# Batched x·yᵀ for 96 heads: groups of four heads with a last tile stored in unequal partition counts, in place of groups of eight heads

## Chip, cores and metric

The kernel runs on one core of a Trainium2 chip. The metric is the device time of one execution in microseconds (us). The core has four compute engines, each with its own instruction queue: TensorE (PE, matrix products), VectorE (DVE) and ScalarE (ACT), which copy and cast, and GpSimd (POOL). SyncE (SP) issues all of this kernel's transfers between HBM and on-chip memory (SBUF); 16 DMA engines carry them out. Matrix products land in PSUM, from where DVE and ACT copy them to SBUF.

## What is computed

```python
def setup_inputs():
    batch, n_heads, seq_t, seq_s, channels = 8, 12, 512, 512, 64
    # x: (8, 12, 512, 64) float32, y: (8, 12, 512, 64) float32

def reference(x, y):
    return np.einsum('bhtc,bhsc->bhts', x, y).astype(np.float32)
```

For each of the 96 heads, a 512×64 matrix times the transpose of another: 512×512 float32 results. 12.6 MB of x and as much of y are read, and 100.7 MB are written.

## The kernel before

A group is eight heads, as two sets `a` of four. In a set, the 128 partitions hold four heads of 32 partitions each; a partition holds 16 consecutive rows of its head (`R`), so each transfer is contiguous in HBM.

**Loads.** `load(g)` (lines 52 to 57) brings 1 MB of y and 1 MB of x, as [128, 2, 16, 64] float32. Three groups are loaded ahead (`AHEAD`).

**`prepare(g)`** (lines 65 to 104) is a generator whose pieces are taken, one at a time, between the matmuls of the group before. POOL casts to bf16 in four instructions (line 73), and each cast puts the same row slot of set 0 and of set 1 side by side, 64 channels each. The next load is queued behind the casts (line 75), since it reuses their buffer. Then PE transposes: 16 slots of y (line 82) and 16 of x (line 95), each a full 128×128, so channels come to lie on partitions, set 0 on 0 to 63 and set 1 on 64 to 127. DVE and ACT copy the transposes from PSUM to `yT` and `xT` (lines 88, 90, 100, 102).

**Products** (lines 109 to 136). For each set, `ot` is a tile of 128 partitions × 16 rows × 512, 4 MB; three such tiles are in rotation. For every pair of row slots, eight matmuls (line 122), each 32 columns of `xT` against 512 of `yT`, fill two PSUM banks `pm`; ACT (line 129) and DVE (line 131) take turns in copying `pm` to `ot`.

**Stores.** A finished `ot` goes out in one DMA of 4 MB (line 136), 32 KB per partition. The first and the last tile go out in four DMAs of 1 MB each (line 134). All loads and stores are on SP's queue in program order. A DMA is issued when its data is there and when the DMA eight places before it, whose completion semaphore it uses again, has landed; the first eight have nothing to wait for in that respect.

Of the kernel before, what the change touches and what calls it, by code (L numbers as in the profile page):

```python
# [1 line left out]

# [5 lines left out]


@with_exitstack  # L10
def kernel(
    ctx: ExitStack,
    tc: tile.TileContext,
    x: bass.AP,
    y: bass.AP,
    out: bass.AP,
):

    nc = tc.nc
    B, H, T, C = x.shape
    _, _, S, _ = y.shape
    P = 128
    G = 4
    Q = P // G
    R = T // Q
    NG = B * H // (2 * G)  # L30
    K = R // 2
    AHEAD = 3
    fp32 = mybir.dt.float32
    bf16 = mybir.dt.bfloat16
    COPY = mybir.ActivationFunctionType.Copy
    assert C * 2 == P and S == T and R == 16

    xv = x.rearrange("b h t c -> (b h t c)").rearrange("(g a p n) -> g p a n", a=2, p=P, n=R * C)
    yv = y.rearrange("b h t c -> (b h t c)").rearrange("(g a p n) -> g p a n", a=2, p=P, n=R * C)
    ov = out.rearrange("b h t s -> (b h t s)").rearrange("(g a p n) -> g a p n", a=2, p=P, n=R * S)  # L40

    const = ctx.enter_context(tc.tile_pool(name="const", bufs=1))
    lpool = ctx.enter_context(tc.tile_pool(name="lpool", bufs=AHEAD))
    bpool = ctx.enter_context(tc.tile_pool(name="bpool", bufs=2))
    tpool = ctx.enter_context(tc.tile_pool(name="tpool", bufs=2))
    opool = ctx.enter_context(tc.tile_pool(name="opool", bufs=3))
    ptpool = ctx.enter_context(tc.tile_pool(name="ptpsum", bufs=2, space=bass.MemoryType.PSUM))
    pmpool = ctx.enter_context(tc.tile_pool(name="pmpsum", bufs=3, space=bass.MemoryType.PSUM))

    loaded = {}  # L50

    def load(g):
        xs = lpool.tile([P, 2, R, C], fp32)
        ys = lpool.tile([P, 2, R, C], fp32)
        nc.sync.dma_start(ys.rearrange("p a r c -> p a (r c)"), yv[g])  # L55
        nc.sync.dma_start(xs.rearrange("p a r c -> p a (r c)"), xv[g])
        loaded[g] = (xs, ys)

    for g in range(AHEAD):
        load(g)  # L60

    ident = const.tile([P, P], bf16)
    make_identity(nc, ident)

    def prepare(g, made):

        xs, ys = loaded.pop(g)
        yb = bpool.tile([P, R, 2, C], bf16)
        xb = bpool.tile([P, R, 2, C], bf16)
        for s, b in ((ys, yb), (xs, xb)):  # L70
            for half in range(2):
                rows = slice(half * K, (half + 1) * K)
                nc.gpsimd.tensor_copy(b[:, rows], s[:, :, rows].rearrange("p a r c -> p r a c"))  # L73
        if g + AHEAD < NG:
            load(g + AHEAD)
        yield
        yT = tpool.tile([P, G * Q, R], bf16)
        xT = tpool.tile([P, R, P], bf16)
        for half in range(2):
            pt = ptpool.tile([P, K, P], bf16)  # L80
            for k in range(K):
                nc.tensor.transpose(  # L82
                    pt[:, k, :], yb[:, half * K + k].rearrange("p a c -> p (a c)"), ident
                )
            dst = yT[:, :, half * K:(half + 1) * K]
            src = pt.rearrange("p k n -> p n k")
            if half == 0:
                nc.vector.tensor_copy(dst, src)  # L88
            else:
                nc.scalar.activation(dst, src, COPY)  # L90
            yield
        for half in range(2):
            pt = ptpool.tile([P, K, P], bf16)
            for k in range(K):
                nc.tensor.transpose(  # L95
                    pt[:, k, :], xb[:, half * K + k].rearrange("p a c -> p (a c)"), ident
                )
            dst = xT[:, half * K:(half + 1) * K]
            if half == 0:
                nc.vector.tensor_copy(dst, pt)  # L100
            else:
                nc.scalar.activation(dst, pt, COPY)  # L102
            yield
        made[g] = (xT, yT.rearrange("p n k -> p (n k)"))

    made = {}
    for _ in prepare(0, made):
        pass
    for g in range(NG):
        xT, yT = made.pop(g)  # L110
        steps = prepare(g + 1, made) if g + 1 < NG else iter(())
        for a in range(2):
            ot = opool.tile([P, R, S], fp32)
            otf = ot.rearrange("p r s -> p (r s)")
            edge = (g == 0 and a == 0) or (g == NG - 1 and a == 1)
            for k in range(K):
                if k in (0, 3, 6):
                    next(steps, None)
                pm = pmpool.tile([P, 2, S], fp32)
                for two in range(2):  # L120
                    for h in range(G):
                        nc.tensor.matmul(  # L122
                            pm[h * Q:(h + 1) * Q, two, :],
                            xT[a * C:(a + 1) * C, 2 * k + two, h * Q:(h + 1) * Q],
                            yT[a * C:(a + 1) * C, h * S:(h + 1) * S],
                            start=True, stop=True,
                        )
                if k % 2 == 0:
                    nc.scalar.activation(ot[:, 2 * k:2 * k + 2, :], pm, COPY)  # L129
                else:  # L130
                    nc.vector.tensor_copy(ot[:, 2 * k:2 * k + 2, :], pm)  # L131
                if edge and k % 2 == 1:
                    i, j = (2 * k - 2) * S, (2 * k + 2) * S
                    nc.sync.dma_start(ov[g, a][:, i:j], otf[:, i:j])
            if not edge:
                nc.sync.dma_start(ov[g, a], otf)  # L136


# [1 line left out]
_INS = ['x', 'y']  # L140
_OUTS = [((8, 12, 512, 512), 'float32')]


# [23 lines left out]
```

## Time and profile before

| | before |
|---|---|
| median of 3 runs | 307.4 us (307.38 to 307.46) |
| profiled execution, its time | 307.38 us |
| profiled execution, its span | 305.6 us |
| PE busy | 203.8 us, 67% |
| DVE busy | 138.4 us, 45% |
| ACT busy | 119.6 us, 39% |
| POOL busy | 49.3 us, 16% |
| bytes moved by DMA | 126.11 MB, mean 413 GB/s |
| DMA packets | 10867 |
| load issued to landed, median | 21.2 us (y), 23.4 us (x) |
| 4 MB store issued to landed, median | 27.4 us |

The span runs from the first to the last instruction; the time holds what lies around it as well. "Busy" of an engine is the sum of its instructions. The page cuts the span in 40 slices and gives for each the busy share of the 16 DMA engines and the rate. A group of instructions is shown with its line, engine, output and input, count, total busy time, mean duration in ns, and the idle time of its engine just before, with what ended most of it. The trace also holds each DMA packet with its start, duration and size, and for each DMA the moments at which its 16 parts landed; neither carries the number of the DMA engine.

### The profile page before, as it was taken

The numbers are of one execution on the slowest core, as the hardware profiler recorded it, in microseconds if no ns is written. First come the engines' busy times: TensorE is split into PE (matmuls) and PEld (weight loads), VectorE is DVE, ScalarE is ACT, GpSimd is POOL, SyncE is SP. The second block draws the span as 40 slices with busy tenths as digits, with TensorE's granted clock in tenths as the row PEclk, the third lists the DMA queues.
The fourth block names the chain that finished last, engine by engine and source line by source line (L and its number), as shares of the span: only waits on it lengthen the run. The fifth ranks groups of instructions, "written<-read, shape, count | busy, mean of one in ns | idle before, by whom it ended". The sixth has DMA issues, their size and how long they took to land.

```text
span 305.6 us, 4378 instructions
## 1 busy us (share of the span) xinstructions
PE 203.8 (67%) x1920; PEld 91.5 (30%) x1920; DVE 138.4 (45%) x120; ACT 119.6 (39%) x121; POOL 49.3 (16%) x54
## 2 busy tenths in 40 slices
PE   1899999969919928936932990991785976575000
PEld 1443234525404503512511540350251432222000
DVE  0465654657416507615633741670664664446000
ACT  1445527544523606505522451560653463325000
POOL 3755024300500500320140050041000000000000
PEclk9999999975555555755675555575575555555555
DMA  7999999999999999999999999999999999999980
GB/s 278 412 409 420 459 419 399 470 418 388 446 455 388 440 446 398 441 429 437 427 424 442 420 427 430 411 454 420 437 435 425 427 442 422 437 437 422 409 368 39
DMA packets 10867, 126.11 MB, mean 413 GB/s; under 512 B 864, under 2 KB 864, under 8 KB 7008
## 3 DMA queue, kind: packets, MB, share of 16 engines
q1 hardware_dynamic: 10848, 125.83, 97.2%
q8 instruction: 15, 0.25, 0.3%
q14 instruction: 4, 0.03, 0.0%
HBM read 25.17 MB, written 100.66 MB: 412 GB/s over the span
## 4 chain that ended last, share of the span: by engine, by line
DMA 49%; PE 29%; DVE 5%; issue 4%; ACT 3%; POOL 1%; SPq 0%; ACTq 0%
DMA out_dram<-ot 47%; PE pm L122 23%; DVE ot L131 5%; PE pt L95 4%; ACT ot L129 3%; PE pt L82 2%; DMA xs<-in_x_dram 2%; ACT xT L102 1%; POOL xb L73 1%; DVE xT L100 0%; SPq L55 0%; ACTq L129 0%; SPq L136 0%
## 5 line engine op out<-in xcount | busy, mean ns | idle before, releaser
L122 PE MATMUL pm<-yT,xT 64*32 64x512 bf16 x1536 | 159.4, 586 | 67.2 <-ACT ot L129 64.7
L131 DVE COPY ot<-pm 128x1024 f32<-128x1024 f32 x96 | 117.0, 1224 | 123.0 <-DMA out_dram<-ot 63.4
L129 ACT ACTIVATE ot<-pm 128x1024 f32<-128x1024 f32 x96 | 95.9, 1023 | 115.5 <-DMA out_dram<-ot 72.1
L122 PEld LDWEIGHTS <-xT 64*32 64x32 bf16 x1536 | 53.3, 118 | 148.1 <-issue 136.3
L73 POOL CAST yb<-ys 128x1024 bf16<-128x1024 f32 x24 | 24.3, 1040 | 143.5 <-PE pt L82 69.8
L82 PE MATMUL pt<-ident,yb 128*128 128x128 bf16 x192 | 23.9, 297 | 8.5 <-POOL yb L73 6.8
L102 ACT ACTIVATE xT<-pt 128x1024 bf16<-128x1024 bf16 x12 | 12.3, 1023 | 37.0 <-PE pt L95 30.3
L95 PE MATMUL pt<-ident,xb 128*128 128x128 bf16 x192 | 25.8, 310 | 1.3 <-DVE xT L100 0.8
L73 POOL CAST xb<-xs 128x1024 bf16<-128x1024 f32 x24 | 24.3, 1040 | 13.7 <-issue 4.9
L95 PEld LDWEIGHTS <-xb 128*128 128x128 bf16 x192 | 19.4, 143 | 22.7 <-issue 20.0
L82 PEld LDWEIGHTS <-yb 128*128 128x128 bf16 x192 | 19.3, 138 | 17.7 <-issue 8.2
L88 DVE COPY yT<-pt 128x1024 bf16<-128x1024 bf16 x12 | 14.6, 1216 | 8.5 <-PE pt L82 8.5
L90 ACT ACTIVATE yT<-pt 128x1024 bf16<-128x1024 bf16 x12 | 12.2, 1019 | 8.2 <-PE pt L82 8.2
L100 DVE COPY xT<-pt 128x1024 bf16<-128x1024 bf16 x12 | 8.3, 690 | 12.3 <-PE pt L95 9.8
L90 ACT ACT_TABLE_LOAD x1 | 1.3, 1283 | 0.7 <-PEq L151 0.7
masks.py:199 POOL TENSOR_SCALAR_AFFINE_SELECT ident<-ident 128x128 bf16<-128x128 bf16 x1 | 0.3, 292 | 0.1
masks.py:197 POOL MEMSET ident<- 128x128 bf16 x1 | 0.2, 204 | 0.3 <-POOLq L151 0.3
L151 POOL MEMSET const-float32-0.0<- 128x1 f32 x1 | 0.1, 98 | 0.2 <-issue 0.2
L151 POOL MEMSET const-bfloat16-1.0<- 128x1 bf16 x1 | 0.1, 101 | 0.0
L151 POOL MEMSET const-uint8-127<- 128x1 uint8 x1 | 0.1, 101 | 0.0
L151 POOL MEMSET const-float32-1.0<- 128x1 f32 x1 | 0.1, 98 | 0.0
## 6 DMA issues: line engine op xcount, KB each, us to landing
out_dram<-ot SPq DMA_DIRECT2D x22, 4096.0 KB, 27.4
ys<-in_y_dram SPq DMA_DIRECT2D x12, 1024.0 KB, 21.2
xs<-in_x_dram SPq DMA_DIRECT2D x12, 1024.0 KB, 23.4
out_dram<-ot SPq DMA_DIRECT2D x8, 1024.0 KB, 19.2
```

What stands on the lines that cost most here:

```text
L73: nc.gpsimd.tensor_copy(b[:, rows], s[:, :, rows].rearrange("p a r c -> p r a c"))
L82: nc.tensor.transpose(pt[:, k, :], yb[:, half * K + k].rearrange("p a c -> p (a c)"), ident)
L88: nc.vector.tensor_copy(dst, src)
L90: nc.scalar.activation(dst, src, COPY)
L95: nc.tensor.transpose(pt[:, k, :], xb[:, half * K + k].rearrange("p a c -> p (a c)"), ident)
L100: nc.vector.tensor_copy(dst, pt)
L102: nc.scalar.activation(dst, pt, COPY)
L122: nc.tensor.matmul(pm[h * Q:(h + 1) * Q, two, :], xT[a * C:(a + 1) * C, 2 * k + two, h * Q:(h + 1) * Q], yT[a * C:(a + 1) * C, h * S:(h + ...
L129: nc.scalar.activation(ot[:, 2 * k:2 * k + 2, :], pm, COPY)
L131: nc.vector.tensor_copy(ot[:, 2 * k:2 * k + 2, :], pm)
L151: nc = _bacc.Bacc("TRN2", target_bir_lowering=False, num_devices=1)
```

## The change

A group is now four heads (`NG` 24 in place of 12). The parts:

- **Loads** are 512 KB each, [128, 1024]; six groups are loaded ahead, with six buffers.
- **Casts.** y is cast in one instruction that writes each row's 64 channels twice, side by side (2048 elements per partition); x is cast as it lies.
- **Transposes.** 16 of y per four heads, each with the same 64 channels on partitions 0 to 63 and on 64 to 127; 8 of x per four heads, each of two consecutive row slots, the even one on partitions 0 to 63 and the odd one on 64 to 127. One DVE copy with a rearranged output writes `xT`, in place of one by DVE and one by ACT.
- **Products.** An `ot` holds two heads: 64 partitions each, 8 rows per partition, 2 MB; eight tiles in rotation. For a `pm`, four matmuls of 64 columns against 512.
- **Stores.** One DMA of 2 MB per tile, 16 KB per partition. The first tile goes out in two DMAs of 1 MB each. The last tile is cut by columns into four pieces of 3, 1, 1.5 and 2.5 times 512 elements; the second is one DMA over 128 partitions; the others are two DMAs each, over 120 and 8, 108 and 20, and 126 and 2 partitions.

```diff
-    NG = B * H // (2 * G)
+    NG = B * H // G
     K = R // 2
-    AHEAD = 3
+    HP = 2
+    I = R // 2
...
-    xv = x.rearrange("b h t c -> (b h t c)").rearrange("(g a p n) -> g p a n", a=2, p=P, n=R * C)
+    xv = x.rearrange("b h t c -> (b h t c)").rearrange("(g p n) -> g p n", p=P, n=R * C)
...
-    ov = out.rearrange("b h t s -> (b h t s)").rearrange("(g a p n) -> g a p n", a=2, p=P, n=R * S)
+    ov = out.rearrange("b h t s -> (b h t s)").rearrange("(g a p n) -> g a p n", a=G // HP, p=P, n=I * S)
...
-    lpool = ctx.enter_context(tc.tile_pool(name="lpool", bufs=AHEAD))
+    lpool = ctx.enter_context(tc.tile_pool(name="lpool", bufs=6))
...
-    opool = ctx.enter_context(tc.tile_pool(name="opool", bufs=3))
+    opool = ctx.enter_context(tc.tile_pool(name="opool", bufs=8))
...
     def load(g):
-        xs = lpool.tile([P, 2, R, C], fp32)
-        ys = lpool.tile([P, 2, R, C], fp32)
-        nc.sync.dma_start(ys.rearrange("p a r c -> p a (r c)"), yv[g])
-        nc.sync.dma_start(xs.rearrange("p a r c -> p a (r c)"), xv[g])
+        xs = lpool.tile([P, R * C], fp32)
+        ys = lpool.tile([P, R * C], fp32)
+        nc.sync.dma_start(ys, yv[g])
+        nc.sync.dma_start(xs, xv[g])
...
         yb = bpool.tile([P, R, 2, C], bf16)
-        xb = bpool.tile([P, R, 2, C], bf16)
-        for s, b in ((ys, yb), (xs, xb)):
-            for half in range(2):
-                rows = slice(half * K, (half + 1) * K)
-                nc.gpsimd.tensor_copy(b[:, rows], s[:, :, rows].rearrange("p a r c -> p r a c"))
-        if g + AHEAD < NG:
-            load(g + AHEAD)
+        nc.gpsimd.tensor_copy(
+            yb, ys.rearrange("p (r c) -> p r c", c=C).unsqueeze(2).to_broadcast([P, R, 2, C])
+        )
+        xb = bpool.tile([P, R * C], bf16)
+        nc.gpsimd.tensor_copy(xb, xs)
+        if g + 6 < NG:
+            load(g + 6)
...
-        xT = tpool.tile([P, R, P], bf16)
+        xT = tpool.tile([P, K // 2, P, 2], bf16)
...
-        for half in range(2):
-            pt = ptpool.tile([P, K, P], bf16)
-            for k in range(K):
-                nc.tensor.transpose(
-                    pt[:, k, :], xb[:, half * K + k].rearrange("p a c -> p (a c)"), ident
-                )
-            dst = xT[:, half * K:(half + 1) * K]
-            if half == 0:
-                nc.vector.tensor_copy(dst, pt)
-            else:
-                nc.scalar.activation(dst, pt, COPY)
-            yield
+        pt = ptpool.tile([P, K, P], bf16)
+        for k in range(K):
+            nc.tensor.transpose(pt[:, k, :], xb[:, k * P:(k + 1) * P], ident)
+        nc.vector.tensor_copy(
+            xT.rearrange("p i n e -> p i e n"), pt.rearrange("p (e i) n -> p i e n", e=2)
+        )
...
-        for a in range(2):
-            ot = opool.tile([P, R, S], fp32)
-            otf = ot.rearrange("p r s -> p (r s)")
-            edge = (g == 0 and a == 0) or (g == NG - 1 and a == 1)
-            for k in range(K):
-                if k in (0, 3, 6):
+        for hp in range(G // HP):
+            ot = opool.tile([P, I, S], fp32)
+            edge = (g == 0 and hp == 0) or (g == NG - 1 and hp == 1)
+            for i2 in range(I // 2):
+                if i2 % 2 == 0:
                     next(steps, None)
                 pm = pmpool.tile([P, 2, S], fp32)
-                for two in range(2):
-                    for h in range(G):
+                for h2 in range(HP):
+                    h = hp * HP + h2
+                    for par in range(2):
                         nc.tensor.matmul(
-                            pm[h * Q:(h + 1) * Q, two, :],
-                            xT[a * C:(a + 1) * C, 2 * k + two, h * Q:(h + 1) * Q],
-                            yT[a * C:(a + 1) * C, h * S:(h + 1) * S],
+                            pm[h2 * 64:(h2 + 1) * 64, par, :],
+                            xT[par * C:(par + 1) * C, i2, h * Q:(h + 1) * Q, :].rearrange("c q e -> c (q e)"),
+                            yT[par * C:(par + 1) * C, h * S:(h + 1) * S],
                             start=True, stop=True,
                         )
...
-                if edge and k % 2 == 1:
-                    i, j = (2 * k - 2) * S, (2 * k + 2) * S
-                    nc.sync.dma_start(ov[g, a][:, i:j], otf[:, i:j])
+                if edge and i2 % 2 == 1:
+                    otf = ot.rearrange("p r s -> p (r s)")
+                    if g == 0:
+                        cuts = [((2 * i2 - 2) * S, (2 * i2 + 2) * S, P)]
+                    elif i2 == 1:
+                        cuts = [(0, 3 * S, 120), (3 * S, 4 * S, P)]
+                    else:
+                        cuts = [(4 * S, 5 * S + S // 2, 108), (5 * S + S // 2, 8 * S, 126)]
+                    for a, b, n in cuts:
+                        nc.sync.dma_start(ov[g, hp][:n, a:b], otf[:n, a:b])
+                        if n < P:
+                            nc.sync.dma_start(ov[g, hp][n:, a:b], otf[n:, a:b])
             if not edge:
-                nc.sync.dma_start(ov[g, a], otf)
+                nc.sync.dma_start(ov[g, hp], ot.rearrange("p r s -> p (r s)"))
```

More of the change, by code (lines that the diff above doesn't have):

```diff
@@ L29 @@
     R = T // Q
-    NG = B * H // (2 * G)
+    NG = B * H // G
     K = R // 2
-    AHEAD = 3
+    HP = 2
+    I = R // 2
     fp32 = mybir.dt.float32
     bf16 = mybir.dt.bfloat16
-    COPY = mybir.ActivationFunctionType.Copy
     assert C * 2 == P and S == T and R == 16
-    xv = x.rearrange("b h t c -> (b h t c)").rearrange("(g a p n) -> g p a n", a=2, p=P, n=R * C)
-    yv = y.rearrange("b h t c -> (b h t c)").rearrange("(g a p n) -> g p a n", a=2, p=P, n=R * C)
-    ov = out.rearrange("b h t s -> (b h t s)").rearrange("(g a p n) -> g a p n", a=2, p=P, n=R * S)
+    xv = x.rearrange("b h t c -> (b h t c)").rearrange("(g p n) -> g p n", p=P, n=R * C)
+    yv = y.rearrange("b h t c -> (b h t c)").rearrange("(g p n) -> g p n", p=P, n=R * C)
+    ov = out.rearrange("b h t s -> (b h t s)").rearrange("(g a p n) -> g a p n", a=G // HP, p=P, n=I * S)
     const = ctx.enter_context(tc.tile_pool(name="const", bufs=1))
-    lpool = ctx.enter_context(tc.tile_pool(name="lpool", bufs=AHEAD))
+    lpool = ctx.enter_context(tc.tile_pool(name="lpool", bufs=6))
     bpool = ctx.enter_context(tc.tile_pool(name="bpool", bufs=2))
     tpool = ctx.enter_context(tc.tile_pool(name="tpool", bufs=2))
-    opool = ctx.enter_context(tc.tile_pool(name="opool", bufs=3))
+    opool = ctx.enter_context(tc.tile_pool(name="opool", bufs=8))
     ptpool = ctx.enter_context(tc.tile_pool(name="ptpsum", bufs=2, space=bass.MemoryType.PSUM))
@@ L52, in load @@
     def load(g):
-        xs = lpool.tile([P, 2, R, C], fp32)
-        ys = lpool.tile([P, 2, R, C], fp32)
-        nc.sync.dma_start(ys.rearrange("p a r c -> p a (r c)"), yv[g])
-        nc.sync.dma_start(xs.rearrange("p a r c -> p a (r c)"), xv[g])
+        xs = lpool.tile([P, R * C], fp32)
+        ys = lpool.tile([P, R * C], fp32)
+        nc.sync.dma_start(ys, yv[g])
+        nc.sync.dma_start(xs, xv[g])
         loaded[g] = (xs, ys)
-    for g in range(AHEAD):
+    for g in range(6):
         load(g)
@@ L89, in prepare @@
             else:
-                nc.scalar.activation(dst, src, COPY)
+                nc.scalar.activation(dst, src, mybir.ActivationFunctionType.Copy)
             yield
-        for half in range(2):
-            pt = ptpool.tile([P, K, P], bf16)
-            for k in range(K):
-                nc.tensor.transpose(
-                    pt[:, k, :], xb[:, half * K + k].rearrange("p a c -> p (a c)"), ident
-                )
-            dst = xT[:, half * K:(half + 1) * K]
-            if half == 0:
-                nc.vector.tensor_copy(dst, pt)
-            else:
-                nc.scalar.activation(dst, pt, COPY)
-            yield
+        pt = ptpool.tile([P, K, P], bf16)
[4 more added lines that the diff above has]
+        )
         made[g] = (xT, yT.rearrange("p n k -> p (n k)"))
+        yield
     made = {}
@@ L126 @@
                             start=True, stop=True,
                         )
-                if k % 2 == 0:
-                    nc.scalar.activation(ot[:, 2 * k:2 * k + 2, :], pm, COPY)
-                else:
-                    nc.vector.tensor_copy(ot[:, 2 * k:2 * k + 2, :], pm)
-                if edge and k % 2 == 1:
-                    i, j = (2 * k - 2) * S, (2 * k + 2) * S
-                    nc.sync.dma_start(ov[g, a][:, i:j], otf[:, i:j])
+                if i2 % 2 == 0:
+                    nc.scalar.activation(ot[:, 2 * i2:2 * i2 + 2, :], pm, mybir.ActivationFunctionType.Copy)
+                else:
+                    nc.vector.tensor_copy(ot[:, 2 * i2:2 * i2 + 2, :], pm)
```

## Prediction

> **What bounds the kernel now.** I read the page's part 2 and 3 first. Columns of part 2: the span in 40 slices, DMA share in tenths and GB/s.
>
> ```profile
> DMA  7999999999999999999999999999999999999980
> GB/s 278 412 409 420 459 419 399 470 418 388 446 455 388 440 446 398 441 429 437 427 424 442 420 427 430 411 454 420 437 435 425 427 442 422 437 437 422 409 368 39
> ...
> q1 hardware_dynamic: 10848, 125.83, 97.2%
> q8 instruction: 15, 0.25, 0.3%
> ```
>
> The 16 DMA engines are full from slice 1 to slice 38; only the first and the last two slices have room. So the time is bytes over DMA rate plus two ends. Next the groups, for what computes beside it:
>
> ```profile
> L122 PE MATMUL pm<-yT,xT 64*32 64x512 bf16 x1536 | 159.4, 586 | 67.2 <-ACT ot L129 64.7
> L131 DVE COPY ot<-pm 128x1024 f32<-128x1024 f32 x96 | 117.0, 1224 | 123.0 <-DMA out_dram<-ot 63.4
> L129 ACT ACTIVATE ot<-pm 128x1024 f32<-128x1024 f32 x96 | 95.9, 1023 | 115.5 <-DMA out_dram<-ot 72.1
> ...
> L73 POOL CAST yb<-ys 128x1024 bf16<-128x1024 f32 x24 | 24.3, 1040 | 143.5 <-PE pt L82 69.8
> ```
>
> DVE and ACT wait mainly for stores to free an `ot`: compute is ahead of the DMA and is throttled by it. Third, the last stores, in windows from 290 us on (last columns: granted clock, DMA share, GB/s):
>
> ```profile
> 290.00:295.00 5.00, 0.00 (x0) 0.00 (x0) 0.00 (x0) 0.00 (x0) 0.00 (x0) 0.50 1.00 423
> 295.00:297.00 2.00, 0.00 (x0) 0.00 (x0) 0.00 (x0) 0.00 (x0) 0.00 (x0) 0.50 0.74 311
> 297.00:298.00 1.00, 0.00 (x0) 0.00 (x0) 0.00 (x0) 0.00 (x0) 0.00 (x0) 0.50 0.50 213
> 298.00:299.00 1.00, 0.00 (x0) 0.00 (x0) 0.00 (x0) 0.00 (x0) 0.00 (x0) 0.50 0.29 123
> 299.00:300.00 1.00, 0.00 (x0) 0.00 (x0) 0.00 (x0) 0.00 (x0) 0.00 (x0) 0.50 0.14 57
> 300.00:301.00 1.00, 0.00 (x0) 0.00 (x0) 0.00 (x0) 0.00 (x0) 0.00 (x0) 0.50 0.06 25
> ...
> 303.00:304.00 1.00, 0.00 (x0) 0.00 (x0) 0.00 (x0) 0.00 (x0) 0.00 (x0) 0.50 0.06 25
> ```
>
> Nothing computes and the engines stop one after another; 0.06 is one engine of 16, alone for the last 4 us. A DMA leaves 16 landing marks in the trace, one per engine. For the last store they read 295.86 (first), six more within 0.93 of it, one at 1.63, six at 2.6 to 3.72, one at 4.66 and the last at 8.79 us behind. So the end is set by one late engine; the span ends 0.96 us after its mark, at 305.6, and the measured 307.4 lies 1.8 above the span.
>
> Two causes of lateness show in the packet records. (1) Of 2816 packets of 32 KB, 2675 took 1210 to 1219 ns and 112 took 1245 to 1321, never two of these at a time: one engine. Each of the 112 lies in a stretch where PE works; while PE idles that engine takes 1213 too. It loses about 65 ns per packet, with some 12.5 matmuls in each: 5 ns per matmul. That engine is the one 8.8 behind. (2) The 15 instruction packets of q8 (16 KB each): after each one, one engine's marks fall 1.4 to 1.8 us back (0.21 to 1.81 after the first). They go round the same eight engines, seven of them hit twice by the end. The late engine is none of the eight.
>
> **The change, part by part.** All sums are made on the landing marks of this execution.
>
> Packets. Loads stay 4 KB per packet, 48 of 512 KB in place of 24 of 1 MB. Stores of 32 KB rows become 16 KB rows. A 4 MB store passes every 9.70 us (8 packets an engine, 1.212 us each), a 1 MB store every 2.45 us (0.306 per 8 KB); on the line between these, 16 KB is 0.608. Two of them cost 1.216, +4 ns for each of 176 packets an engine: +0.7 us. The pieces stored in 8 KB packets drop from two 4 MB tiles to one 2 MB tile and the last tile: −0.1. DMAs rise from 54 to 103, each with one 9 ns packet of 4 B on each engine: +0.4. An engine with no hit would land its last store at 295.86 + 1.0 = 296.9.
>
> Late engine. Matmuls fall from 1920 (1536 and 384 transposes) to 1344 (768 of 64 columns, 576 transposes, since `yb` now doubles each row and gives 16 transposes per 4 heads). By matmuls, 8.8 × 0.70 = 6.2 us late. Bounds: 4.4 if line 122's matmuls alone count (they halve), 8.8 if nothing changes.
>
> Instruction packets. PE's list falls from 3842 to 2690 rows. 15 packets fit 256 rows each, so 10 remain: two engines are hit twice. A twice-hit engine is 2.6 to 4.66 behind now; I take 3.7, the top of the close group of six.
>
> Last tile. 2 MB, 128 KB an engine if even, 16 × 0.306 = 4.9 us. Seven of its eight columns (3 + 1.5 + 2.5 of S) go by stores of 120, 108 and 126 rows plus remainders of 8, 20 and 2. No row of this trace is a store of other than 128 rows. In those each engine moves whole rows, 8 of them. Nearest to that, 120 rows are 15 engines of 8, and 108 and 126 are 12 and 14 engines of 9. An engine left out of all three saves 7/8 × 4.9 = 4.3 us; one that takes a ninth row in two and rows of remainders has 20 to 26 KB more, at 27 GB/s (32 KB in 1.21) 0.8 to 0.9 us. Ends: −4.3 if the late engine is the one left out, +0.9 if not. I take −4.3 for the forecast and keep the other as rival A. The far bound on the bad side is a store confined to a single engine (25 GB/s in the tail rows): 720 KB would take 29 us. I give that no weight, since 16 marks come from every store seen.
>
> [...]
>
> Sum: late engine 296.9 + 6.2 − 4.3 = 298.8. Twice-hit engine with extra rows: 296.9 + 3.7 + 0.8 = 301.4, now the last. Plus 0.96 and 1.8: **304.2 us**. With 2.6 and no extra rows 302.3; with 4.66 and 0.9, 305.2.
>
> [...] Row: four 1 MB stores in a full queue pass 2.45 us apart, 428 GB/s, with no pause between DMAs. [...]
>
> **Costed at nothing, with the cover.** Per 8 MB of output the DMA needs about 24.4 us (two 9.70 and two loads of 2.5). Work beside it, same 8 MB: DVE 8 × 1.224 + 2 × 1.216 + 2 × (0.69 to 1.22) = 14 to 15; ACT 8 × 1.023 + 2 × 1.02 = 10; POOL two `xb` of 1.04 and two doubled `yb` of 1.04 to 2.08 = 4 to 6; PE 48 transposes at 0.13 (8 in 1.01) = 6, and 64 matmuls at 0.107 to 0.214 (8 in 0.86) = 7 to 14. All fit. If one passed 24.4, the excess would count twelve times. Start: both queue 6 MB of loads first. The twelve now wait on one another eight back (4 MB in flight, 10 us), and the load of group 6 waits for the casts of group 0, that of group 7 for those of group 1; the first stores queue behind both. Landing marks of xs for group 0 come 2.6 us earlier (1 MB less ahead), so I see no hole; a hole costs its length. End: seven issues of 0.33 us are 2.3 on SP, but with eight `ot` of 2 MB they are issued some 30 us before they move. The 2-row store waits for the tile two before the last to land everywhere: hidden while the late engine is under some 9 us behind (4.9 for a tile plus the pieces queued).
>
> **Rivals.** A: the late engine isn't relieved (it is not the one left out, or it is the source rows in SBUF that are slow, whoever moves them). 296.9 + 6.2 + 0 to 0.9 = 303.1 to 304.0, time 305.9 to 306.8. For: no mark names an engine. If in addition it still loses 8.8, 308.5 to 309.4.
>
> B, slower: rows handed out in eights and nines put two engines on the same part of SBUF and they take turns. Price: 4.3 us of odd-shaped packets stretched. Nearest row: an instruction packet of 16 KB, sharing its engine, took 0.98 us (0.3% of 16 engines × 305.6 over 15) against 0.608 alone, 1.6 times; full turn-taking is 2 times. 1.6 gives +2.6, 306.8; 2 gives +4.3, 308.5. It decides from 1.75 times on (3.2 us). For it: even 128-row stores run at just 27 GB/s an engine, with nothing in the trace on what limits that. Against: engines are up to 4 us apart, so turns need not coincide. [...]
>
> C: the odd packets are stretched by 1.25 to 1.6 times only: 305.3 to 306.8.
>
> **Chances.** Forecast 0.48; A as priced 0.17; A with 8.8 kept 0.06; C 0.12; B 0.17. About 0.2% (0.6 us) is what a measurement of this kernel can tell. Faster (below 306.8): forecast, most of A and C, 0.70. Same (to 308.0): 0.09, edges of A and B. Slower: 0.21. Forecast's own range 302.3 to 305.3; held 8 times in 10: 302.6 to 308.4.
>
> **What would show it.** Right: landing marks of the last stores within 5 us of the first, no single engine alone for over 1.5 us; 10 or 11 packets on q8; 103 DMAs; 16 KB packets near 0.61 us; the slow packets fewer. Wrong: a tail of 0.06 shares of 4 us (A), packets of 5 or 6 KB well above 0.2 us (B), or slices under 9 in the middle (a cover that failed).

## The result: 1.4% slower, and the profile after

The changed kernel takes 311.8 us, the median of 4 runs (311.36 to 312.27), against 307.4 for the kernel before (4 runs, 307.38 to 307.59): ratio 1.0142, 95% interval 1.0124 to 1.0159. The forecast was 304.2. Executions more than 1.5% above the fastest of their kernel count as slow and are left out of all ratios; this bears on two of run 5 alone. The profiled execution took 312.08 with a span of 309.9, 4.3 more than before; the other 0.4 lies around the span.

First the same two parts of the page as before: the DMA engines' busy tenths and rate in 40 slices, and the queues.

```profile
DMA  7999999999999999999999999999999999999960
GB/s 291 416 383 435 425 416 434 425 422 427 426 433 427 411 445 423 421 436 421 432 427 421 436 424 422 436 427 422 432 434 427 432 427 431 429 434 431 406 195 26
...
q1 hardware_dynamic: 14413, 125.84, 96.9%
q8 instruction: 10, 0.16, 0.2%
```

The middle is as full as before, at 411 to 445 GB/s from slice 3 to slice 36 (counted from 0), so no cover failed there. Ten packets on q8, as forecast. But slice 38 says 6 tenths busy at 195 GB/s, while a full slice moves about 425: engines that are busy and move less than their share of time would give. Before, the same slice had 8 tenths and 368 GB/s. Next the groups:

```profile
L125 DVE COPY ot<-pm 128x1024 f32<-128x1024 f32 x96 | 116.3, 1220 | 78.9 <-DMA out_dram<-ot 59.0
L123 ACT ACTIVATE ot<-pm 128x1024 f32<-128x1024 f32 x96 | 94.4, 1022 | 141.8 <-DMA out_dram<-ot 129.6
L116 PE MATMUL pm<-yT,xT 64*64 64x512 bf16 x768 | 96.3, 566 | 89.0 <-ACT ot L123 71.3
L68 POOL CAST yb<-ys 128x2048 bf16<-128x2048 f32 x24 | 45.4, 1893 | 134.8 <-DMA ys<-in_y_dram 113.2
```

The copies still wait mostly for stores, ACT now 129.6 us of its idle time: compute is still ahead of the DMA. The doubled cast costs 1893 ns, inside its bounds. What is left is the end. The windows from 290 us on, changed kernel (last two columns: DMA share, GB/s):

```profile
290.00:295.00 5.00, 0.00 (x0) 0.00 (x0) 0.00 (x0) 0.00 (x0) 0.00 (x0) 0.50 0.98 380
295.00:297.00 2.00, 0.00 (x0) 0.00 (x0) 0.00 (x0) 0.00 (x0) 0.00 (x0) 0.50 0.92 230
297.00:298.00 1.00, 0.00 (x0) 0.00 (x0) 0.00 (x0) 0.00 (x0) 0.00 (x0) 0.50 0.81 256
299.00:300.00 1.00, 0.00 (x0) 0.00 (x0) 0.00 (x0) 0.00 (x0) 0.00 (x0) 0.50 0.56 155
303.00:304.00 1.00, 0.00 (x0) 0.00 (x0) 0.00 (x0) 0.00 (x0) 0.00 (x0) 0.50 0.11 45
305.00:306.00 1.00, 0.00 (x0) 0.00 (x0) 0.00 (x0) 0.00 (x0) 0.00 (x0) 0.50 0.06 25
306.00:308.00 2.00, 0.00 (x0) 0.00 (x0) 0.00 (x0) 0.00 (x0) 0.00 (x0) 0.50 0.06 26
```

A fully busy set moves about 425 GB/s (426 at a share of 0.99 from 285 to 290). From 295 to 297 the engines are 0.92 busy and move 230: 0.92 of 425 would be 391, so packets take about 1.7 times as long. And one engine is alone from about 304 to 308.6 (a share of 0.06, 25 to 26 GB/s).

The packet records say which. After 291 us 70 packets took over 60 ns longer than their size takes elsewhere, 25.2 us in all (they are called stretched below); six of them are 16 KB packets that should take 611 ns and took 1.02 to 2.6 us. The engine that ends last can be followed backwards: it finishes its part of the tile before the last at 302.96, then takes 8 packets of 6 KB, one more of 6 KB, 8 of 2 KB, 9 and 2 of 3 KB, 9 of 5 KB, and ends at 308.9. So the late engine was left out of none of the cut stores but the 2-row one, and moved five rows more than its share (one of 6 KB, three of 3 KB, one of 5 KB): 148 KB in place of 128. On the tile before that its mark (294.42) lay 7.5 us behind the first, its lag; one tile on it lay 11.2 behind, where an undisturbed tile of 4.86 us would have kept it at 7.5.

### The profile page after: what moved, and what is told of

It reads as the page before. It is cut to its first block, busy times and chain, and to the rows that moved or that the text cites. A ratio compares the mean times of both kernels' runs of the same rounds, so it can differ in the third digit from the quotient of the medians.

```text
span 309.9 us, 3414 instructions
## 1 busy us (share of the span) xinstructions
PE 154.4 (50%) x1344; PEld 81.7 (26%) x1344; DVE 172.7 (56%) x144; ACT 117.5 (38%) x121; POOL 70.6 (23%) x54
## 2 busy tenths in 40 slices
DMA packets 14428, 126.04 MB, mean 407 GB/s; under 512 B 1613, under 2 KB 1613, under 8 KB 8269
## 4 chain that ended last, share of the span: by engine, by line
DMA 70%; DVE 10%; PE 3%; issue 2%; ACT 1%; POOL 1%; SPq 0%; ACTq 0%
DMA out_dram<-ot 69%; DVE ot L125 7%; DVE xT L94 2%; PE pm L116 2%; DVE yT L87 1%; DMA ys<-in_y_dram 1%; ACT ot L123 1%; PE pt L81 1%; POOL yb L68 1%; PE pt L93 0%; SPq L139 0%; ACTq L123 0%
## 5 line engine op out<-in xcount | busy, mean ns | idle before, releaser
L123 ACT ACTIVATE ot<-pm 128x1024 f32<-128x1024 f32 x96 | 94.4, 1022 | 141.8 <-DMA out_dram<-ot 129.6
L116 PE MATMUL pm<-yT,xT 64*64 64x512 bf16 x768 | 96.3, 566 | 89.0 <-ACT ot L123 71.3
L68 POOL CAST yb<-ys 128x2048 bf16<-128x2048 f32 x24 | 45.4, 1893 | 134.8 <-DMA ys<-in_y_dram 113.2
L116 PEld LDWEIGHTS <-xT 64*64 64x64 bf16 x768 | 32.1, 122 | 136.6 <-issue 118.6
L81 PE MATMUL pt<-ident,yb 128*128 128x128 bf16 x384 | 41.5, 269 | 17.6 <-DVE xT L94 11.2
L81 PEld LDWEIGHTS <-yb 128*128 128x128 bf16 x384 | 33.4, 125 | 25.7 <-issue 19.6
L94 DVE COPY xT<-pt 128x1024 bf16<-128x1024 bf16 x24 | 31.1, 1298 | 9.5 <-PE pt L93 9.5
L87 DVE COPY yT<-pt 128x1024 bf16<-128x1024 bf16 x24 | 29.1, 1214 | 7.2 <-PE pt L81 7.2
L89 ACT ACTIVATE yT<-pt 128x1024 bf16<-128x1024 bf16 x24 | 24.7, 1028 | 7.2 <-PE pt L81 6.4
L93 PEld LDWEIGHTS <-xb 128*128 128x128 bf16 x192 | 17.3, 125 | 22.5 <-issue 22.5
```

Source lines behind the costliest of these rows:

```text
L68: nc.gpsimd.tensor_copy(yb, ys.rearrange("p (r c) -> p r c", c=C).unsqueeze(2).to_broadcast([P, R, 2, C]))
L81: nc.tensor.transpose(pt[:, k, :], yb[:, half * K + k].rearrange("p a c -> p (a c)"), ident)
L89: nc.scalar.activation(dst, src, mybir.ActivationFunctionType.Copy)
L93: nc.tensor.transpose(pt[:, k, :], xb[:, k * P:(k + 1) * P], ident)
L94: nc.vector.tensor_copy(xT.rearrange("p i n e -> p i e n"), pt.rearrange("p (e i) n -> p i e n", e=2))
L116: nc.tensor.matmul(pm[h2 * 64:(h2 + 1) * 64, par, :], xT[par * C:(par + 1) * C, i2, h * Q:(h + 1) * Q, :].rearrange("c q e -> c (q e)"), y ...
```

## Experiments

Two theories. **T**: the unequal stores make engines read the same parts of SBUF and slow one another, the late engine above all, and give the late engine more rows. **R**: the rest of the change (finer packets, smaller loads, groups of four) costs the 4 us. All diffs but the third and the eighth are against the changed kernel.

**1. The cut undone.**

```diff
-                    elif i2 == 1:
-                        cuts = [(0, 3 * S, 120), (3 * S, 4 * S, P)]
-                    else:
-                        cuts = [(4 * S, 5 * S + S // 2, 108), (5 * S + S // 2, 8 * S, 126)]
+                    cuts = [((2 * i2 - 2) * S, (2 * i2 + 2) * S, P)]
```

> The changed kernel, with its last tile in two 1 MB stores over 128 partitions. Theory T (the unequal stores make engines wait on one another for the same part of SBUF, and give the late engine more rows besides): the late engine's mark for the tile two before the end was 294.4; two tiles of 4.86 more give 304.1, span 305.1, time 306.9 to 307.4. Theory R (the rest of the change costs the 4 us: finer packets, 512 KB loads, groups of four): 310.5 to 312. Late engine's lag on the last store: T 7.5 us as on the tiles before, with no packet of 16 KB above 700 ns outside instruction fetches.

Measured: 307.55 us, median of 11 runs (306.79 to 311.27), ratio 1.0018 (0.9989 to 1.0048). R falls: without the cut no difference from the kernel before shows. The median lies just above the 306.9 to 307.4 expected. In the profiled execution, after 284 us, all 225 packets of 16 KB took 611 ns and all 256 of 8 KB took 309. Its windows over the same stretch:

```profile
290.00:295.00 5.00, 0.00 (x0) 0.00 (x0) 0.00 (x0) 0.00 (x0) 0.00 (x0) 0.50 1.00 426
295.00:297.00 2.00, 0.00 (x0) 0.00 (x0) 0.00 (x0) 0.00 (x0) 0.00 (x0) 0.50 0.92 389
297.00:298.00 1.00, 0.00 (x0) 0.00 (x0) 0.00 (x0) 0.00 (x0) 0.00 (x0) 0.50 0.62 262
299.00:300.00 1.00, 0.00 (x0) 0.00 (x0) 0.00 (x0) 0.00 (x0) 0.00 (x0) 0.50 0.16 66
303.00:304.00 1.00, 0.00 (x0) 0.00 (x0) 0.00 (x0) 0.00 (x0) 0.00 (x0) 0.50 0.14 57
```

Share and rate fall together here (0.92 and 389, against 0.92 and 230 with the cut): engines stop, but none is slowed. One thing was not as expected: three engines, not one, end 7.4 to 8.1 behind in this execution. One of them drifts steadily through the run, to 7.4 behind; the marks of the other two fall back in steps, as after instruction packets (1.4 to 1.8 us each in the kernel before). That the hits fall differently from run to run, and make the spread of 4.5 us in the times, is likely but not shown, since one trace of this kernel is kept.

**2. Stores of 64 + 64 rows.** The last tile's two pieces as four stores (`n = 64`): 4 rows for each engine, if 16 share the rows evenly.

> The changed kernel with each 1 MB piece of its last tile stored as 64 + 64 partitions, so every engine keeps its share of bytes if 64 rows go over 16 engines (4 each), and no engine is left out or loaded more. Theory T in the form that rows of one part of SBUF can't be read by two engines at full rate: 64 rows lie in half of the parts, packets of 8 KB go from 0.31 to about 0.6 us, the last 2 MB take up to 4.9 us longer: 309 to 312. Rival N (only the number of rows per engine matters, engines do not disturb one another): the same as with 128 partitions, 306.9 to 307.5, packets at 0.31 us.

Measured: 310.5 us (309.99 to 312.15), ratio 1.0109 (1.0084 to 1.0134), 2.9 us over the even end, with 52 stretched packets, 19.7 us in all. If the shares are equal, they alone are not it; N falls.

**3. The cut in the kernel before.** On the last 2 MB of its last tile.

```diff
-                    nc.sync.dma_start(ov[g, a][:, i:j], otf[:, i:j])
+                    if g == 0 or k < 4:
+                        cuts = [(i, j, P)]
+                    elif k == 5:
+                        cuts = [(i, i + 3 * S, 120), (i + 3 * S, j, P)]
+                    else:
+                        cuts = [(i, i + S + S // 2, 108), (i + S + S // 2, j, 126)]
+                    for i, j, n in cuts:
+                        nc.sync.dma_start(ov[g, a][:n, i:j], otf[:n, i:j])
+                        if n < P:
+                            nc.sync.dma_start(ov[g, a][n:, i:j], otf[n:, i:j])
```

> The kernel before, its last 2 MB (of the last 4 MB tile) in the unequal stores; nothing else changed. T: slower by what it costs in the changed kernel, 3.5 to 5.5 us: 311 to 313. R: no more than 1 us either way.

Measured: 311.5 us (311.14 to 311.67), ratio 1.0129 (1.0113 to 1.0144): 4.1 us, 72 stretched packets. The same price in the other kernel.

**4. Which engine is late.** An even end, but 512 B of each row of the last tile go out first, in stores of 3, 4, 6, 7 and 108 rows.

> The changed kernel with an even last tile, but its first 512 B per partition stored by five small stores of 3, 4, 6, 7 and 108 partitions. [...] Time about that of the even tail plus under 1 us.

Landing marks, us, in the trace of this run:

```
3 rows:  292.10 292.83 293.02
4 rows:  292.27 293.01 293.20 294.94
6 rows:  292.45 293.18 293.37 294.24 295.12 299.23
7 rows:  292.63 293.36 293.42 293.55 294.44 295.31 299.42
```

The late mark (299.2) is there with 6 rows and not with 4: the late engine takes part in the stores of 6 and 7 rows and not in those of 3 and 4, whose last marks are 293.02 and 294.94. This is the engine whose lag grows steadily through the run, to 7.1 on the tile before the last. Each of the four stores left as many marks as it has rows, and each mark comes again in the next store, 0.17 to 0.20 us later, which reads as the same engines taking part again. In the changed kernel the seven stores of the last tile, of 120, 8, 128, 108, 20, 126 and 2 rows, left 15, 8, 16, 12, 10, 14 and 2 marks, and the last engine's chain is in all of them but the 2-row one. The counts agree: the 4-byte completion packets of the changed kernel are 1613, which is 103 × 16 less the 35 that 15, 8, 12, 10, 14 and 2 marks leave out. The trace gives no engine a number; that the late engine of this run and that of the changed kernel are the same one is likely from their steady lags (7.1 and 7.5 us), but not shown.

The time, 309.6 (two runs), is 2 us over the even end, more than expected: no packet is stretched here, but the engines ran dry near 296 (41% busy from 295 to 297). The five small stores hold five of the eight completion semaphores, and the two big stores behind them each waited for a whole tile to land on the last engine (issued at 292.0 and 296.9). In this execution that was yet another engine, 9.8 behind, whose lag had grown in steps, as after instruction packets; its mark is in none of the five small stores, the 108-row one included. The forecast had costed that wait at nothing; in the changed kernel no such dip shows (a share of 0.98 from 290 to 295 us).

**5. Half-height stores in the middle.** The even kernel, eight 2 MB tiles (groups 10 to 13) as 64 + 64 rows.

> The even kernel (changed kernel with two 1 MB stores at the end), with eight 2 MB tiles in the middle (groups 10 to 13) each stored as 64 + 64 partitions, 16 KB per row as before; shares of the engines stay equal. If engines that read rows of the same part of SBUF take turns wherever it happens: a 64-row store of 1 MB takes up to 4.9 us in place of 2.4, so up to 9.7 a tile; engines that stand apart in time escape part of it. 1 to 4.9 us for each of eight tiles: 316 to 347, with packets of 16 KB at 0.9 to 1.2 us in that stretch. If the disturbance only arises at the end, beside a late engine's backlog: 307 to 309, packets at 0.61.

Measured: 312.8 and 315.7 us, ratio 1.0221 (1.0179 to 1.0263); two more executions took 325.2 and 326.0. So 5 to 8 us for eight tiles, 0.7 to 1.0 each, a little under the 1 to 4.9 expected, with no tail near. Between 146 and 200 us 119 packets of 16 KB took over 670 ns, 1.09 us in the mean; in the even kernel two did. The windows of this run in that stretch, and then those of the even kernel:

```profile
140.00:150.00 10.00, 5.21 (x45) 2.88 (x42) 5.38 (x5) 4.11 (x5) 1.92 (x2) 0.50 1.01 411
150.00:160.00 10.00, 6.21 (x48) 3.43 (x45) 5.70 (x5) 2.62 (x3) 2.06 (x2) 0.50 1.01 327
160.00:170.00 10.00, 3.48 (x29) 2.05 (x29) 3.85 (x4) 2.85 (x3) 2.08 (x2) 0.50 1.00 383
```

```profile
140.00:150.00 10.00, 5.51 (x44) 3.22 (x43) 5.40 (x5) 2.63 (x3) 1.09 (x2) 0.50 1.02 430
150.00:160.00 10.00, 6.68 (x52) 3.88 (x52) 6.65 (x6) 4.10 (x5) 2.93 (x2) 0.50 1.02 426
160.00:170.00 10.00, 5.08 (x44) 2.87 (x44) 5.57 (x5) 3.48 (x4) 2.93 (x2) 0.67 0.99 419
```

DMA share 1.01 and 1.02, 327 GB/s against 426. The disturbance does not need the end of the run. Whether it needs an engine that lags was not tried: one was already 4 us behind at 145 us. Why it varies so much from run to run was not settled.

**6. Equal shares, other rows.** The last tile's pieces as 112 + 16 rows. All 100 DMAs of this kernel have their 16 completion packets (1600 of 4 bytes); shared evenly, that is 7 rows and 1 row for each of 16 engines.

> The changed kernel with each 1 MB piece of its last tile stored as 112 + 16 partitions: 7 and 1 rows for each of 16 engines, so equal shares and all engines in use, but rows other than in a 128-row store. Theory T (who reads which rows matters): 309 to 311, stretched packets as with 64 + 64 (2.9 us there). Theory S (the cost of the change came from unequal shares, the late engine's extra rows): 306.8 to 307.8.

Measured: 310.8 us (310.50 to 312.68), ratio 1.0121 (1.0096 to 1.0146), 66 stretched packets with 29.6 us. All engines in use, shares equal if the rows are shared evenly, and 3.2 us lost: S falls.

**7. What makes one engine late.** The even kernel with every transpose of y done twice (`for k in range(2 * K)`, index `k % K`).

> The even kernel with each transpose of y done twice into the same place (384 more PE matmuls, 1728 in place of 1344, and as many weight loads). If the late engine loses about 5 ns for each PE matmul: its packets of 16 KB lose 6.8 us x 1.29 = 8.7 us in all (6.8 in the even kernel), and its lag at the end grows by about 1.9; 3 more instruction packets on q8 (13). If it loses by stores or by time: 6.8 us as before, lag 7.4 to 8.1.

Measured: 308.8 us (308.55 to 308.85), 13 packets on q8. The slightly slow 16 KB packets (3 ns to 140 over 611; nearly always one at a time, while PE works) lose 8.4 us in all, against 6.8 in the even kernel and 5.4 in run 8. Per matmul that is 4.9, 5.1 and 4.7 ns. The last engine's lag is 9.3. PE's busy time does not order the three: 161, 157 and 204 us. Each matmul has its own weight load (1344 of each on the page of the changed kernel), so the two are not told apart.

**8. Fewer matmuls.** The kernel before, with 64-column matmuls and 2 MB tiles.

```diff
-    opool = ctx.enter_context(tc.tile_pool(name="opool", bufs=3))
+    opool = ctx.enter_context(tc.tile_pool(name="opool", bufs=6))
...
-        xT = tpool.tile([P, R, P], bf16)
+        xT = tpool.tile([P, K, P, 2], bf16)
...
-            dst = xT[:, half * K:(half + 1) * K]
+            dst = xT[:, :, :, half]
...
-        for a in range(2):
-            ot = opool.tile([P, R, S], fp32)
+        for t in range(4):
+            a, hp = t // 2, t % 2
+            ot = opool.tile([P, K, S], fp32)
...
+                    for h2 in range(HP):
+                        h = hp * HP + h2
                         nc.tensor.matmul(
-                            pm[h * Q:(h + 1) * Q, two, :],
-                            xT[a * C:(a + 1) * C, 2 * k + two, h * Q:(h + 1) * Q],
+                            pm[h2 * 64:(h2 + 1) * 64, two, :],
+                            xT[a * C:(a + 1) * C, 2 * i2 + two, h * Q:(h + 1) * Q, :].rearrange("c q e -> c (q e)"),
                             yT[a * C:(a + 1) * C, h * S:(h + 1) * S],
```

> Groups of eight heads and loads as in the kernel before, with 64-column matmuls, 2 MB tiles of two heads and six of them in rotation, even stores at both ends: 1152 matmuls (768 and 384 transposes) in place of 1920 and 1344, 9 instruction packets. If the late engine goes by PE's matmuls its lag is 5.5 to 6.5 us, at the packets' cost of 16 KB rows (+0.7): 305.5 to 306.5. If it does not: 307 to 308.

Measured: 306.1 us (305.79 to 306.61), ratio 0.9959 (0.9946 to 0.9973), lag 6.3 us: 1.4 us better than the kernel before, and better than the changed one by 5.8. It takes from the change the 64-column matmuls, half as many, without its extra transposes and without the cut. It also has 2 MB tiles and six instruction packets fewer than the kernel before, so the 1.4 us is not shown to be the matmuls' alone; the lag, 8.8 before and 6.3 here, is what their count forecast.

```profile
q1 hardware_dynamic: 13728, 125.83, 98.3%
q8 instruction: 9, 0.15, 0.2%
```

Its DMA share is 98.3%, against 97.2 before: the end is more even.

**9 and 10. The rows themselves.** The last tile in two stores of 64 rows, the rest of that tile left out: once rows 0 to 63, once rows 32 to 95.

```diff
+                    p0, p1 = (0, P) if g == 0 else (32, 96)
+                    nc.sync.dma_start(ov[g, hp][p0:p1, a:b], otf[p0:p1, a:b])
```

> The changed kernel, of whose last tile only partitions 0 to 63 are stored, in two stores of 64 rows; the other half of that tile is left out. [...] Bytes alone would end 2.4 us before the even kernel's 307.5, at 305.1; with the disturbance 306 to 308.

> As the run before, but partitions 32 to 95 are stored and the rest left out: the same bytes, row count and share of each engine. [...] If the disturbance comes from 64-row stores as such, from HBM's side or from the number of stores, both runs are alike.

Measured: 307.6 us with rows 0 to 63 (10 runs, 306.66 to 308.25), 305.2 with rows 32 to 95 (10 runs, 304.46 to 308.90). Windows of the first:

```profile
292.00:294.00 2.00, 0.00 (x0) 0.00 (x0) 0.00 (x0) 0.00 (x0) 0.00 (x0) 0.50 1.02 360
294.00:296.00 2.00, 0.00 (x0) 0.00 (x0) 0.00 (x0) 0.00 (x0) 0.00 (x0) 0.50 0.98 246
296.00:298.00 2.00, 0.00 (x0) 0.00 (x0) 0.00 (x0) 0.00 (x0) 0.00 (x0) 0.50 0.56 143
```

and of the second:

```profile
292.00:294.00 2.00, 0.00 (x0) 0.00 (x0) 0.00 (x0) 0.00 (x0) 0.00 (x0) 0.50 0.96 410
294.00:296.00 2.00, 0.00 (x0) 0.00 (x0) 0.00 (x0) 0.00 (x0) 0.00 (x0) 0.50 0.55 234
296.00:298.00 2.00, 0.00 (x0) 0.00 (x0) 0.00 (x0) 0.00 (x0) 0.00 (x0) 0.50 0.35 147
```

With rows 0 to 63, 62 packets are stretched by 30.2 us in all, and an 8 KB packet takes 501 ns in the mean. With rows 32 to 95 none is: all 128 take 309 ns, and rate and share fall together (234 GB/s at 0.55). (The profiled execution with rows 32 to 95 is its longest, 308.9: one engine was 11.9 us behind on the tile before already, with no packet stretched.) Same bytes, same row count, same number of stores: what counts is which rows they are. That engines meet at parts of SBUF and slow one another there, as T has it, is not shown, nor in which parts rows lie: no trace says where a slowed packet waits.

## Why the prediction was wrong, step by step

- **Packets and the undisturbed engine: right.** 296.9 was forecast for the first engine's last mark; the tile before the last has its first mark at 291.78, and with an even tile of 4.86 that is 296.6 (296.66 in run 1).
- **Late engine, 8.8 × 0.70 = 6.2 us: right in kind, too low.** 7.5 measured. Runs 7 and 8 fit PE's matmuls (or their weight loads) as the driver at 4.7 to 5.1 ns each on 16 KB packets; but the kernel before lost only 7.5 us on its 32 KB packets, 3.9 ns per matmul over 1920, so scaling its lag by count was wrong by 1.3 us.
- **Instruction packets: right in number and size, not in place.** Ten, as forecast. On the last tile that the cut did not touch, three engines, not two, stood at 3.6 to 3.9 behind, where 3.7 was taken for a twice-hit one. "Round the same eight engines" did not hold in run 1.
- **Last tile, "I take −4.3 for the forecast": the step that failed.** It chose the engine left out to be the late one. No row showed that, and the prediction said so. No run shows the −4.3, nor the share-out of rows behind it and behind the +0.8. The late engine was left out of the 2-row store alone; it was not relieved at all, and it got rows on top, 20 KB: from 302.96 to 308.93 it needed 5.97 us where an even share takes 4.9, +1.1, of which 0.2 are two stretched packets.
- **Rival B: right that packets are stretched, with its price too small.** It put the stretch of the cut's own packets at up to 4.3 us and came to 308.5. That two engines take turns on the same part of SBUF, as it supposed, is not shown. What it missed is that the late engine's queued 16 KB packets of the tile before are slowed as well: 11.2 behind in place of 7.5, +3.7, which four packets of 1.02 to 2.6 us in its chain account for. What these packets met, the trace does not say. With 1.1 for the last tile, 4.8 us on the end. The medians differ by 4.3 from the even kernel, whose own end was set by another engine, 8.1 behind, and by 4.1 in run 3. Both signs that the prediction named for A and B came: the tail at 0.06, and packets of 5 and 6 KB at up to 0.65 and 1.8 us.
- **Rival A, the late engine not relieved,** forecast 305.9 to 306.8 without B. It holds too, together with B; the prediction had treated the two as alternatives. Priced together by its own figures, 306.8 + 4.3, they come to 311.1.
- **Cost per DMA: the number of stores does not order the losses.** Seven stores at the end in place of two lose 4.3 us in the changed kernel and 2 in run 4; four lose 2.9 in run 2 and 3.2 in run 6; runs 9 and 10, two stores each, differ by 2.4.
- **Cover: right, with one wrong detail.** The middle slices are full. It is closest at the start, where DVE is busy for all of 20 to 50 us, with the DMA share still at 1.00 to 1.01. The last cut stores were not issued some 30 us ahead: three went out at 284.7, 289.6 and 294.4, each as the DMA eight places before it landed. No hole came of it: the DMA share is 0.98 from 290 to 295 us.
- **Two slips without weight.** The DMA row before is full up to slice 37 counted from 0 (slice 38 has 8), and 20 to 26 KB at 27 GB/s are 0.8 to 1.0 us, not 0.8 to 0.9.

In short: the late engine's last mark was forecast at 298.8 and came at 308.93. Of the 10.1 us between, 4.3 are the relief that did not come, 3.7 its slowed packets, 1.1 its last tile, 1.3 its larger lag, less 0.3 for an earlier first mark. Without the cut the medians differ by 0.1 us, within the interval; the cut costs 4.3.

## What to carry to other kernels

At an end that waits for one DMA engine, first find out which engine it is; a store of few rows helps by the marks that it leaves (in run 4 the late mark, 299.2, came with 6 rows and not with 4). Whether moving that engine's work to others pays was not tried here, since the cut gave it more. What the runs show is that a cut store can slow the very engine that is late: in the changed kernel four of its 16 KB packets took 1.02 to 2.6 us in place of 0.611. The unequal stores, 112 + 16 and 64 + 64 rows stretched 70, 66 and 52 packets, while the whole 128-row stores of run 1 stretched none (8 KB in 309 ns), nor did rows 32 to 95 in run 10. Here a high DMA share at a low rate was the sign of it (0.92 at 230 GB/s); in run 1 the share fell along with the rate (0.62 at 262 GB/s), and engines were plainly idle. Fewer matmuls, with whole stores, did pay here: 1.4 us in run 8.

## What the runs showed of the hardware that was not expected

- One DMA engine is slowed while PE works: 16 KB mostly in 620 to 660 ns in place of 611, about 5 ns for each matmul (4.7 to 5.1 in the even kernel and runs 7 and 8), and 384 matmuls more cost it 1.6 us more on its packets (8.4 against 6.8). By what path was not tried, nor whether the profiler's own records of PE's instructions have a part in it.
- What a 64-row store takes goes by its rows: rows 0 to 63 took 501 ns per 8 KB packet (run 9), rows 32 to 95 took 309 (run 10), as in the 128-row stores of run 1.
- In kernels that are the same up to their last tile, the lags that grow in steps, as after instruction packets, come out differently: before that tile the three latest engines lagged by 3.9, 3.9 and 7.5 us in the changed kernel, 7.4, 7.7 and 8.1 in run 1, and 5.2, 7.1 and 9.8 in run 4. This would explain why the even kernel spreads from 306.8 to 311.3 us, while the kernel before, whose last engine stood 4 us clear of the hit ones, stays within 307.3 to 307.7 over 15 runs; it is not shown, as one trace of each kernel is kept.
